# Four of the eight plain weight pieces of an output projection become seven products

## The chip, the cores and the metric

The kernel runs on one core of one Trainium2 chip. The metric is the device time of one execution in microseconds (us). TensorE multiplies, VectorE and ScalarE do the elementwise work, GpSimd's queue (POOL in the profile) issues the adding transfers, and SyncE's queue (SP) issues the plain loads from HBM.

## The reference, cut to what matters

One layer with 256 tokens and a model width of 2048. A first projection feeds two groups of eight heads: `fox` (forgetting attention) and `sb` (stick-breaking attention). Their outputs are normalised group by group and projected, and a gated feed-forward follows:

```
merged = concatenate([rms_norm(out_a, out_norm_fox), rms_norm(out_b, out_norm_sb)])   # 256 x 2048
x = x + merged @ w_out                                                                # w_out 2048 x 2048
x = x + conv_ffn(rms_norm(x, ffn_norm))
```

The change is in `merged @ w_out`, in the part that `out_b` feeds: 256 tokens x 1024 inner x 2048 columns.

## The kernel before

**Three passes for one product.** Every weight piece is 128 partitions x 2048 values. ScalarE writes a rounded copy (`w_hi`, L263) and VectorE the rest (`w_lo = raw - w_hi`, L271). A product is then data high x `w_hi`, data low x `w_hi`, data high x `w_lo`: three matmuls of 512 columns where one would do in full precision. A plain piece of `w_out` covers four heads (4 x 128 inner) and 512 columns, and serves both token tiles: 4 x 3 x 2 = 24 matmuls.

**Seven instead of eight.** For a block of 1024 inner x 1024 columns x 256 tokens the kernel elsewhere uses a scheme of seven products with twelve matmuls each, instead of four plain pieces with twenty-four (84 matmuls for 96). It needs sums of the data blocks, sums of the weight blocks (made by adding transfers on POOL's queue or by VectorE), and one update of `x2` from PSUM for each product. `out_unit` does this for columns 0 to 1023 of the fox heads (group 0).

**The order of work.** The program is a list of steps, one weight piece each. In the iteration of step n the loop at the end of the file emits, in this order: one round of the pending follow-ups (`following`), the split of step n+2's weights, another round of the follow-ups, the load of step n+6, the matmuls of step n, one round of `after` (the transposes), and one tick of the attention heads still running. A follow-up is a generator: each round runs it up to its next `yield`. Each engine works its own instructions strictly in this order. There are five raw weight buffers, three of `w_hi` and three of `w_lo`.

**PSUM.** Eight banks: two double tiles from the pool `psa` (`acc_tile`: plain pieces of the sb heads, later the feed-forward) and a pool `psb` of four single banks with tag `t` (heads, transposes, small sums).

**The stage that is changed.** For the sb heads (group 1) there are eight plain pieces, `out_rows(1, c, kh)`: column block c (512 columns) and head half kh, in the order (0,0) (1,0) (0,1) (1,1) (2,0) (2,1) (3,0) (3,1). Head 7 finishes inside (0,1). After (0,1), `norm_of_heads` turns the sums of squares into the factor `rg1`. Then, once per column block, `follow` adds the two accumulators to `x2` (two VectorE instructions, L989), `next_rows(c)` transposes the finished block on TensorE (eight transposes into two `ps_x` banks, L192), `squares` sums its squares on ScalarE (L210), and `rows_split` evicts the transposes into `hT` as high halves (ScalarE, L200) and low halves (VectorE, L203), one pair of `hT` tiles, a `yield`, then the other pair; after tiles 12 to 15 there is no `yield`. `hT` tiles 4c to 4c+3 are the inner rows of the feed-forward. Its first step uses tiles 0 to 7, its second 8 to 15, in two halves.

Of the kernel before, what the change touches and what calls it, by code (L numbers as in the profile page):

```python
# [45 lines left out]
def hybrid_layer(  # L46
# [731 lines left out]
    def sb_head(h, half):  # L778
# [47 lines left out]
            oSb.append(rows_tile(f"oSb{h}", 0 if h >= 4 else 1, F32R).rearrange("p (a s) -> p a s", a=2))  # L826
        o = oSb[h]
        act.activation(o[:, 0, :], po, AF.Identity, scale=g_sb[:, h : h + 1])
# [36 lines left out]
        ts = slice(t * P, (t + 1) * P)  # L865
        return lambda i, p, _: fox_cells[p][:, 4 * n + i, ts]

    def out_unit(c0):
        w11, w12, w21, w22 = (rows_of(wo, 4 * h, 4, c0 + n * 512, 512) for h in range(2) for n in range(2))
        mem, bank = {}, {}  # L870

        def product(name, new, lhs, weights, to, load_=(), sums=None, plus=None, negative=False, first=False, then=None):
            parts = []
            n, t = to

            def loads():
                for key, src in load_:
                    mem[key] = load(src)
                if plus is not None:
                    nc.gpsimd.dma_start(  # L880
                        mem[weights].rearrange("p (a b) -> p a b", a=4), plus, accum_op=ALU.add
                    )

            def prepare():
                parts.extend(split(mem[weights], 4, 512))

            def matmuls():
                if new:
                    bank[name] = bank_tile(f"bank_{name}", 2 + "ab".index(name[0]))
                in_three([bank[name]], parts, 4, lhs, new, True)  # L890
                if first:
                    following.append(norm_of_heads(0, rgs[0]))
                    next(following[-1])

            def follow():
                while "rg0" not in ready:
                    yield
                xs = x2[:, t, c0 + n * 512 : c0 + (n + 1) * 512]
                r = (nrg0 if negative else rgs[0])[:, t : t + 1]
                dve.scalar_tensor_tensor(xs, bank[name], r, xs, op0=ALU.mult, op1=ALU.add)  # L900
                if then:
                    then()

            new_step(loads, sums, prepare, matmuls, follow)

        def sum_of(other):
            return lambda: dve.tensor_tensor(mem["11"], mem["11"], mem[other], op=ALU.add) and None

        yield product("a", True, of_raw(0, 0), "11", (0, 0), [("11", w11)], first=True)
        yield product("bc", True, of_raw(1, 0), "21", (0, 0), [("21", w21)], then=sum_of("22"))  # L910
        yield product("b", True, fox_sum(T5), "11", (1, 1), [("12", w12)], sum_of("12"))
        yield product("a", False, fox_sum(S2), "11", (1, 0), [("22", w22)], negative=True)
        yield product("b", False, fox_sum(S4), "22", (1, 0))
        yield product("a", False, fox_sum(T7), "12", (1, 1), plus=w22, negative=True)
        yield product("a", False, of_raw(1, 1), "11", (0, 1), plus=w21)

    def split_fox(h):
        act.copy(hT[:, h : h + 4, 0, :], oFox[:, h : h + 4, :])
# [5 lines left out]
    def norm_of_heads(group, rg):  # L924
        pg = psb.tile([P, NT], F32, name="pg", tag="t")
        for t in range(NT):
            nc.tensor.matmul(
                pg[:, t : t + 1], ssq[group][:, t * P : (t + 1) * P], ones[:, 0:1],
                start=t == 0, stop=t == NT - 1,
            )  # L930
        yield
        yield from rsqrt(rg, pg, 1.0 / WF, NT, 2 - group)
        if group == 0:
            dve.tensor_scalar(nrg0, rg, -1.0, None, op0=ALU.mult)
        ready.add(f"rg{group}")

    rgs = [const.tile([P, NT], F32, name=f"rg{i}") for i in range(2)]
    nrg0 = const.tile([P, NT], F32, name="nrg0")
    rstd2 = const.tile([P, NT], F32, name="rstd2")

    def next_rows(c):
# [18 lines left out]
    def out_rows(group, c, kh):  # L960

        def matmuls(parts):
# [14 lines left out]
                middle=finish_heads if flush else middle, apart=1 if flush else 0,  # L977
            )
            if kh == 1 == group and c == 0:
                following.append(norm_of_heads(group, rgs[group]))  # L980
                next(following[-1])

        def follow():
            acc = cells[c]
            while f"rg{group}" not in ready:
                yield
            for t in range(NT):
                xs = x2[:, t, c * 512 : (c + 1) * 512]
                dve.scalar_tensor_tensor(  # L989
                    xs, acc[t], rgs[group][:, t : t + 1], xs, op0=ALU.mult, op1=ALU.add  # L990
                )
            while group == 0 and held:
                held.pop()()
            if group == 1:
                after.append(next_rows(c))
                yield
                if c == 0:
                    spare.append(heads_tile("spare").rearrange("p a b -> p (a b)")[:, :512])
                squares(ss2, c, spare[1])
                if c == 3:  # L1000
                    for _ in token_factors(rstd2, ss2):
                        pass
                    for t in range(NT):
                        dg2.append(R2[:, t * P : (t + 1) * P])
                        dve.tensor_scalar(dg2[t], ident, rstd2[:, t : t + 1], None, op0=ALU.mult)

        pieces(
            wo, group * NH + 4 * kh, 4, 512 * c, 512, matmuls, follow if kh else None,
            held if (group, c, kh) == (0, 3, 0) else None,
        )  # L1010

    dg2 = []
    held = []
    ORDER = [None, (2, 0), None, (2, 1), None, (3, 0), None, None, None, (3, 1), None]
    unit0 = out_unit(0)
# [111 lines left out]
    def up_pieces(part, f0, follows):  # L1127
# [4 lines left out]
        def piece(kh):  # L1132
# [10 lines left out]
            def matmuls():  # L1143
# [1 line left out]
                    cell.append(acc_tile("pu"))  # L1145
                acc, (hi, lo) = cell[0], mem["parts"]
                first = kh and part.f_lo == f0 == 0 and follows is gate_follows
                halves = (range(4), range(4, 8)) if first else (range(8),)
                order = (0, 1) if first else lows
                for ks, low, j in [(ks, low, j) for ks in halves for low in order for j in range(2)]:  # L1150
                        for i in ks:
                            k = 8 * kh + i
                            nc.tensor.matmul(  # L1153
                                acc[:, j, S:] if low else acc[:, j, :],
                                (lo if low else hi)[:, i, j * P : (j + 1) * P],
                                hT[:, k, 0, :] if low else hT[:, k].rearrange("p a b -> p (a b)"),
                                start=k == 0 and not low, stop=k == KT - 1 and low == order[1],
                            )

            new_step(loads, None, prepare, matmuls, (lambda: follows(part, cell[0], f0)) if kh else None)  # L1160
# [174 lines left out]
    def begin(task):  # L1335
        next(task)
        after.append(task)
# [81 lines left out]
```

## Time and profile before

| | |
|---|---|
| three runs, median (lowest to highest) | 1094.4 us (1093.81 to 1095.0) |
| the profiled execution, first to last instruction | 1091.8 us |
| TensorE, VectorE, ScalarE busy | 1087.3, 924.2, 755.1 us |
| granted TensorE clock, mean | 0.999 |
| DMA, mean | 237 GB/s |

The profiled execution has its own time, the span from the first to the last instruction; the runs' time has the launch around it, so the two are compared with their difference in mind. Matmuls overlap, so TensorE's busy share says only that it rarely stands; the chain of waits says when it stands and for whom.

### The profile page before, as it was taken

The page shows a single profiled execution, that of the slowest core. Times are in us where ns is not written, and L with a number is a line of the kernel's source. Part 1 is how long each engine was busy: PE and PEld are TensorE (multiplying, and loading weights), DVE is VectorE, ACT ScalarE, POOL GpSimd, SP SyncE. Part 2 cuts the span into 40 slices and gives each one's busy share as a digit, 9 for nine tenths or more (in the row PEclk, how much of TensorE's full clock was granted, in tenths as well). Part 3 has the DMA queues.
Part 4 walks back from the last instruction along what each step waited for, and adds up shares of the span by engine and source line. Part 5 has one row for each costly group of instructions (what it writes and reads, how often), then busy time and mean ns, then how long its engine had stood idle before and what let it go on. Part 6 is the DMA issues. An engine that isn't in the chain of part 4 may idle for free.

```text
span 1091.8 us, 14685 instructions
## 1 busy us (share of the span) xinstructions
PE 1087.3 (100%) x5701; PEld 939.5 (86%) x5701; DVE 924.2 (85%) x918; ACT 755.1 (69%) x968; POOL 59.0 (5%) x53
## 2 busy tenths in 40 slices
PE   9999999999999999999999999999999999999998
PEld 9988888888888888888888888888888888888887
DVE  5988899888897667779887988889898889879996
ACT  6767697767766657767766776677667767667763
POOL 0000000001000000000000000100000000000000
PEclk9999999999999999999999999999999999999999
DMA  8897886868777465669989597996969799896995
GB/s 310 276 272 239 271 206 196 253 183 271 239 214 251 154 199 161 214 170 249 288 206 316 173 265 254 254 296 170 302 195 271 241 246 279 215 319 161 291 247 155
DMA packets 175215, 258.53 MB, mean 237 GB/s; under 512 B 4632, under 2 KB 98218, under 8 KB 175146
## 3 DMA queue, kind: packets, MB, share of 16 engines
q1 hardware_dynamic: 151690, 210.26, 56.9%
q0 software_dynamic: 23280, 47.19, 24.5%
q8 instruction: 45, 0.74, 0.3%
q14 instruction: 24, 0.20, 0.1%
q10 hardware_dynamic: 176, 0.14, 0.0%
HBM read 255.48 MB, written 2.10 MB: 236 GB/s over the span
## 4 chain that ended last, share of the span: by engine, by line
PE 100%; DVE 0%; issue 0%
PE pu L1153 45%; PE bank_a L291 18%; PE bank_b L291 11%; PE bank_c L291 6%; PE acc_o L291 6%; PE acc_v L411 4%; PE bank_e L291 2%; PE acc L291 2%; PE ps_x L192 1%; PE ps_h L637 1%; PE ps_o L709 1%; PE ps_z L785 0%; PE ps_o L710 0%; PE ps_z L805 0%; PE ps_i L186 0%; PE half L291 0%
## 5 line engine op out<-in xcount | busy, mean ns | idle before, releaser
L271 DVE TENSOR_TENSOR w_lo<-w_raw,w_hi 128x2048 fp32r<-128x2048 f32 (+2 forms) x251 | 555.9, 2219 | 124.1 <-ACT w_hi L263 123.1
L263 ACT CAST w_hi<-w_raw 128x2048 fp32r<-128x2048 f32 (+2 forms) x251 | 464.6, 1854 | 220.7 <-PE pu L1153 90.0
L1153 PE MATMUL pu<-hT,w_hi 128*128 128x512 f32 x1408 | 333.6, 390 | 0.0
L1153 PEld LDWEIGHTS pu<-hT,w_hi 128*128 128x128 f32 x1408 | 263.1, 188 | 53.6
L1153 PEld LDWEIGHTS pu<-hT,w_lo 128*128 128x128 f32 x1408 | 180.0, 191 | 6.5
L1153 PE MATMUL pu<-hT,w_lo 128*128 128x256 f32 x1408 | 182.1, 283 | 0.0
L1206 POOL DMA_DIRECT2D w_raw<-in_w_down_dram x31 | 39.8, 1302 | 715.9 <-DVE w_lo L271 384.7
L1078 ACT ACTIVATE tap<-up,ccol 128x256 f32<-128x256 f32 x176 | 74.6, 495 | 0.0
L291 PE MATMUL bank_a<-w_hi,hT 128*128 128x512 f32 x192 | 48.5, 395 | 0.0
L291 PEld LDWEIGHTS bank_a<-w_hi,hT 128*128 128x128 f32 x192 | 35.2, 188 | 6.7
L291 PE MATMUL bank_b<-w_hi,s 128*128 128x512 f32 x160 | 40.1, 393 | 0.0
L291 PE MATMUL bank_a<-w_hi,s 128*128 128x512 f32 x160 | 40.0, 392 | 0.0
L291 PE MATMUL bank_a<-w_hi,g 128*128 128x512 f32 x152 | 38.0, 392 | 0.0
L411 PE MATMUL acc_v<-w_hi,hT 128*128 128x344 f32 x192 | 35.7, 328 | 0.0
L291 PEld LDWEIGHTS bank_b<-w_hi,s 128*128 128x128 f32 x160 | 28.8, 189 | 5.5 <-issue 0.3
L291 PEld LDWEIGHTS bank_a<-w_hi,s 128*128 128x128 f32 x160 | 28.9, 189 | 5.2
L1083 DVE TENSOR_TENSOR gate<-gate,tap 128x512 f32<-128x512 f32 x44 | 30.3, 689 | 2.7 <-DVE gate L1083 0.5
L1083 DVE TENSOR_TENSOR val<-val,tap 128x512 f32<-128x512 f32 x44 | 30.3, 689 | 2.3
L291 PE MATMUL acc_o<-w_hi,oSb 128*128 128x512 f32 x128 | 31.8, 397 | 0.0
L1064 DVE TENSOR_TENSOR up<-t,R 128x512 f32<-128x512 f32 x44 | 30.5, 692 | 1.5
L291 PEld LDWEIGHTS bank_a<-w_hi,g 128*128 128x128 f32 x152 | 27.4, 189 | 4.9
L411 PEld LDWEIGHTS acc_v<-w_hi,hT 128*128 128x128 f32 x192 | 30.4, 190 | 0.5 <-DVE hT L203 0.2
(293 smaller groups left out, 1411.2 us busy)
## 6 DMA issues: line engine op xcount, KB each, us to landing
w_raw<-in_w_up_dram SPq DMA_DIRECT2D x88, 1024.0 KB, 7.0
w_raw<-in_w_down_dram SPq DMA_DIRECT2D x44, 1024.0 KB, 6.7
w_raw<-in_w_in_dram SPq DMA_DIRECT2D x40, 1024.0 KB, 5.5
w_raw<-in_w_down_dram POOLq DMA_DIRECT2D x31, 1024.0 KB, 9.8
w_raw<-in_w_out_dram SPq DMA_DIRECT2D x16, 1024.0 KB, 7.7
w_raw<-in_w_in_dram POOLq DMA_DIRECT2D x10, 1024.0 KB, 9.4
w_raw<-in_w_in_dram SPq DMA_DIRECT2D x13, 516.0 KB, 5.5
xb<-in_x_dram POOLq DMA_DIRECT2D x4, 512.0 KB, 8.7
```

The source lines that it names most:

```text
L192: nc.tensor.transpose(ps[:, j, t * P : (t + 1) * P], x2[:, t, (k + j) * P : (k + j + 1) * P], ident)
L263: copy(hi[:, :n], raw[:, :n])
L271: dve.tensor_tensor(lo[:, :n], raw[:, :n], f32(hi[:, :n]), op=ALU.subtract)
L291: nc.tensor.matmul(o, lhs(i, l, t), r[:, i, :] if cut is None else r[:, i, cut], start=starts and j == 0, stop=stops and j == 3 * n - 1, s ...
L411: nc.tensor.matmul(banks[j][t][:, :VC], of_half(hT[:, k], l, t), w[:, 0, m * VC : (m + 1) * VC], start=k == l == 0 and w is mem["parts", i ...
L637: nc.tensor.transpose(ps[:, h, :], rows[n, t][:, h * HD : (h + 1) * HD], ident)
L709: mm(po, v, w[:, i, :S], start=m == 0, stop=False)
L1064: dve.tensor_tensor(u[:, :, 2:], t2, R, op=ALU.mult)
L1078: act.activation(taps[w][:, j, :], u[:, j, w : w + S], AF.Copy, scale=ccol[:, w, f : f + 1])
L1083: dve.tensor_tensor(a, a, tap, op=ALU.add)
L1153: nc.tensor.matmul(acc[:, j, S:] if low else acc[:, j, :], (lo if low else hi)[:, i, j * P : (j + 1) * P], hT[:, k, 0, :] if low else hT[: ...
L1206: nc.gpsimd.dma_start(mem[weights].rearrange("p (a b) -> p a b", a=4), plus, accum_op=ALU.add)
```

## The change

It gives columns 1024 to 2047 of the sb heads to `out_unit`, which takes a group, a first column and a function for the raw data tiles now. The eight steps become eleven:

| step | what it multiplies | weights | matmuls |
|---|---|---|---|
| 1 | product a, raw data (heads 0-3, tokens 0-127) | w11 | 12 |
| 2, 3, 4 | plain (0,0), (1,0), (0,1) | own | 24 each |
| 5 | product b, T5 | w11+w12 (adding transfer) | 12 |
| 6 | product bc, raw data (heads 4-7, tokens 0-127) | w21 | 12 |
| 7 | product a, S2 | w11+w12+w22 (VectorE adds w22) | 12 |
| 8 | plain (1,1) | own | 24 |
| 9 | product a, T7 | w12+w22 (adding transfer) | 12 |
| 10 | product b, S4, finishes column block 3 | w22 | 12 |
| 11 | product a, raw data (heads 0-3, tokens 128-255), finishes column block 2 | w11+w12+w22+w21 (adding transfer) | 12 |

The three accumulators a, b and bc come from `psb` (tag `t`). `sb_head` writes heads 4 to 7 once more, whole, into `oFox`; heads 0 to 3 are put together there by VectorE (`sums_of_first_heads`, begun in step 4's iteration). `sums_of_heads` makes the data sums and their high and low halves in five rounds: the first at the end of step 4, with the VectorE sum of w22 into w11 behind it, the others in the rounds of steps 5, 6 and 7. `norm_of_heads` gives `rg1` in one round now. The follow-up of (0,1) has one more `yield` ahead of its two adds and two more behind them. Block 2 is now the last to be finished, so the feed-forward's second step takes tiles 12 to 15 ahead of 8 to 11.

```
+        if h >= 4:
+            act.activation(oFox[:, h, :], po, AF.Identity, scale=g_sb[:, h : h + 1])
...
+        def open_bank(name):
+            if group == 0:
+                return bank_tile(f"bank_{name}", 2 + "ab".index(name[0]))
+            return psb.tile([P, 512], F32, name=f"bank_{name}", tag="t")
...
+        else:
+            yield product("b", True, fox_sum(T5), "11", (1, 1), plus=w12)
+            yield c()
+            weight_sum.append(sum_of("22"))
         yield product("a", False, fox_sum(S2), "11", (1, 0), [("22", w22)], negative=True)
...
+        yield product("a", False, fox_sum(T7), "12", (1, 1), [("12", w12)] if group else (), plus=w22, negative=True)
+        if group:
+            yield s4(3)
+        yield product("a", False, raw_tokens(1, 1), "11", (0, 1), plus=w21, finished=2 if group else None)
...
+        yield from rsqrt(rg, pg, 1.0 / WF, NT, 0 if group else 2)
+        dve.tensor_scalar(nrgs[group], rg, -1.0, None, op0=ALU.mult)
...
             if kh == 1 == group and c == 0:
-                following.append(norm_of_heads(group, rgs[group]))
+                following.extend((norm_of_heads(group, rgs[group]), sums_of_heads()))
+                next(following[-2])
                 next(following[-1])
...
+            if group > c:
                 yield
             for t in range(NT):
                 xs = x2[:, t, c * 512 : (c + 1) * 512]
...
+            if group > c:
+                yield
+                yield
             if group == 1:
-                after.append(next_rows(c))
...
+                yield from columns_done(c)
...
+    def sums_of_heads():
+        a11, a21 = oFox[:, first_heads, first_tokens], oFox[:, first_heads, last_tokens]
+        a12, a22 = oFox[:, last_heads, first_tokens], oFox[:, last_heads, last_tokens]
+        dve.tensor_tensor(a21, a21, a22, op=ALU.subtract)
+        high_sum(first_heads, last_tokens)
+        dve.scalar_tensor_tensor(a22, a11, -1.0, a22, op0=ALU.mult, op1=ALU.subtract)
+        low_sum(first_heads, last_tokens)
+        weight_sum.pop()()
+        yield
+        high_sum(last_heads, last_tokens)
+        low_sum(last_heads, last_tokens)
+        dve.tensor_tensor(a12, a12, a22, op=ALU.add)
+        yield
+        high_sum(last_heads, first_tokens)
+        high_sum(first_heads, first_tokens)
+        yield
+        low_sum(first_heads, first_tokens)
+        yield
+        yield
+        low_sum(last_heads, first_tokens)
...
-    for c, kh in ((0, 0), (1, 0), (0, 1), (1, 1), (2, 0), (2, 1), (3, 0), (3, 1)):
-        out_rows(1, c, kh)
+    SB_OUT = len(steps)
+    unit1 = out_unit(1, 1024, of_heads)
+    for what in (None, (0, 0), (1, 0), (0, 1), None, None, None, (1, 1), None, None, None):
+        if what is None:
+            next(unit1)
+        else:
+            out_rows(1, *what)
...
-                halves = (range(4), range(4, 8)) if first else (range(8),)
+                halves = (range(4, 8), range(4)) if first else (range(8),)
...
+    hooks[SB_OUT + 2] = lambda: following.append(sums_of_first_heads())
```

`high_sum` is a ScalarE copy and `low_sum` a VectorE subtraction of 128 x 512 values; `columns_done` holds what stood at the end of `follow` (transposes, squares, and after the last block the token factors).

More of the change, by code (lines that the diff above doesn't have):

```diff
@@ L888, in matmuls @@
                 if new:
-                    bank[name] = bank_tile(f"bank_{name}", 2 + "ab".index(name[0]))
+                    bank[name] = open_bank(name)
                 in_three([bank[name]], parts, 4, lhs, new, True)
@@ L902, in follow @@
                     then()
+                if finished is not None:
+                    yield from columns_done(finished)
             new_step(loads, sums, prepare, matmuls, follow)
@@ L1156, in matmuls @@
                                 hT[:, k, 0, :] if low else hT[:, k].rearrange("p a b -> p (a b)"),
-                                start=k == 0 and not low, stop=k == KT - 1 and low == order[1],
+                                start=k == 0 and not low, stop=bool(kh) and k == last_k and low == order[1],
                             )
```

77 lines of the change are left out of this document (50 added, 27 removed).

## The prediction

> **What bounds the kernel now.** I read the page's busy shares and its chain first, then the chain in order of time through the stage, then the busy time by stretch, then VectorE's timeline. TensorE is the whole chain:
>
> ```profile
> span 1091.8 us, 14685 instructions
> PE 100%; DVE 0%; issue 0%
> ...
> 314.73 2.75 PE bank_a L291 x12
> ...
> 340.98 5.52 PE acc_o L291 x24
> ...
> 347.60 0.98 PE acc_o L291 x4
> 348.58 0.43 PE ps_o L821 x2
> 349.01 0.22 PE ps_o L822 x2
> 349.23 4.58 PE acc_o L291 x20
> 353.81 0.34 PE pg L927 x4
> ...
> 366.25 0.87 PE ps_x L192 x8
> ...
> 384.38 5.54 PE pu L1153 x32
> 389.92 0.87 PE ps_x L192 x8
> 390.79 5.59 PE pu L1153 x32
> ```
>
> A product of 12 matmuls takes 2.75 us, a plain piece of 24 takes 5.5, with nothing between them. So a matmul left out is worth its 0.229 us, and any time for which TensorE stands is lost whole. The question is whether VectorE can still feed it:
>
> ```profile
> 284.70:334.40 49.70, 49.70 (x244) 41.78 (x244) 48.29 (x55) 35.21 (x43) 2.60 (x2) 1.00 0.77 228
> 334.40:384.40 50.00, 50.00 (x244) 41.80 (x243) 34.12 (x47) 29.75 (x48) 0.00 (x0) 1.00 0.53 173
> ...
> PEld ps_x L192 <- DVE xb L989: 0.3, 1, 0.3
> ```
>
> The columns are stretch, length, busy us of TensorE, weight loads, VectorE, ScalarE, POOL, then clock and DMA. The first row holds the seven products of the fox heads: VectorE is busy for 48.29 of 49.70 us there, and TensorE doesn't stand. The second row is the stage that changes: 34.12 of 50.00. The last row matters most: TensorE already waits 0.3 us for the adds of column block 0 ahead of their transposes. There is no slack at that place.
>
> **What is saved.** Four plain pieces (96 matmuls) become seven products (84): 12 x 0.229 = 2.7 us less on TensorE. Transposes and feed-forward matmuls keep their number.
>
> **What VectorE gets, and its prices.**
>
> ```profile
> 308.24 4.49 DVE L271 TENSOR_TENSOR w_lo<-w_raw,w_hi 128x2048 fp32r<-128x2048 f32 x2
> ...
> 350.45 0.41 DVE L834 TENSOR_TENSOR ssq<-ssq,osq 128x256 f32<-128x256 f32 x1
> 354.19 0.16 DVE L168 TENSOR_SCALAR rs_a<-pg 128x2 f32<-128x2 f32 x1 [3.32 <-PE pg L927]
> ...
> 357.55 0.15 DVE L173 TENSOR_TENSOR rs_u<-rs_a,rs_y 128x2 f32<-128x2 f32 x1
> 357.73 0.16 DVE L174 TENSOR_TENSOR rs_u<-rs_u,rs_y 128x2 f32<-128x2 f32 x1
> ...
> 358.33 1.41 DVE L989 SCALAR_TENSOR_TENSOR xb<-acc_o,rg,xb 128x512 f32<-128x512 f32 x2
> 361.35 0.88 DVE L203 SCALAR_TENSOR_TENSOR hT<-ps_x,pcol,hT 128x256 fp32r<-128x256 f32 x2 [1.61 <-ACT hT L200]
> ...
> L907 DVE TENSOR_TENSOR w_raw<-w_raw 128x2048 f32<-128x2048 f32 x2 | 4.6, 2282 | 0.0
> L853 DVE TENSOR_TENSOR oFox<-oFox 128x512 f32<-128x512 f32 x1 | 0.7, 694 | 0.0
> ```
>
> Two splits last 4.49 us while one row is 2.29: behind one another, an instruction starts 0.09 us before the row ahead of it ends. Queue prices are then: split or weight sum 2.20, update of `x2` 0.66 (from the pair of 1.41), `hT` low half 0.40, a sum of 128 x 512 0.60, the 128x2 steps of the norm 0.20. Added: three splits 6.6, one weight sum 2.2, three updates 2.0, seven sums in `sums_of_heads` 4.2, the sums of the first heads 1.9 (four of half width, one of 0.60). That is 16.9 us on 34.1, in a stage of 47.3: over 100% before any wait. So what counts is where the overflow lies in the strict order.
>
> **The place: transposes of block 0.** I walk the queues from head 7. Up to (0,1) the new stage has 12 matmuls more (12+24+24 for 24+24), so (0,1) starts at 347.60 + 2.75 = 350.35. TensorE then has 24 matmuls with head 7's 0.65 between them, the 0.34 of `pg`, and steps 5 and 6: 350.35 + 0.98 + 0.65 + 4.58 + 0.34 + 5.5 = 362.4. There the transposes of block 0 are due. VectorE's last work on head 7 began 2.85 us after (0,1)'s start (350.45 - 347.60); with the extra `oFox` copy ahead of it on ScalarE (0.36, estimated from the row of 0.47 below) it is free for the sums at 353.9. In emission order follow: three sums with a wait for ScalarE's copy (2.0), the weight sum (2.2), the norm (six small steps and ScalarE's two, 1.7), two sums (1.2), the split for step 7 with its wait for the cast (2.4), the update of step 1 and the two adds of (0,1) (2.0). That is 11.5 us: 365.5. The adds stand behind all of it since the added `yield` lets the split go first. **TensorE waits 3.1 us** where it waited 0.3 (ends 2.1 and 3.6: the queue without its small waits, and with as much again on ScalarE's side); nothing hides it, since step 7 is queued behind these transposes. The first sums do not hurt: step 5 needs them at 356.9 and has them at 355.9.
>
> **The second place: the banks.** `psb` has four banks. When `next_rows(0)` is emitted, behind step 6, a, b and bc hold three: bc's update comes only in step 7's iteration. The eight transposes need two. The second four must wait until the first bank is given back, which is behind the low halves of the first pair. VectorE's queue up to there: a sum 0.60, the update of step 5 0.66, the split for step 8 2.20, a sum 0.60, two low halves 0.88: 4.9 us, 370.4, against 366.0 when the first four transposes are through: **4.4 us**. The trace has only short waits of this kind:
>
> ```profile
> PEld ps_h L637 <- ACT kB L641: 0.2, 1, 0.2
> ```
>
> Zero is the lower end (if the allocation finds a bank), 5.1 the upper (if it is bc's bank that comes free, one update later); I take 4.4, since the pair's bank is given back first.
>
> **Then it catches up.** Step 8 is long, and VectorE is through its splits before (1,1) ends. From there VectorE has, up to the add that finishes block 3: two adds 1.3, two splits 4.4, four low halves 1.6, two updates 1.3 and about 1.0 of waits for ScalarE: 9.6 us, beside 9.1 of TensorE (three products and eight transposes 0.87). It waits **0.9 us** ahead of block 3's transposes (0.5 by the plain difference; the rest is the lag of matmul ends).
>
> **The last place: block 2 in the feed-forward's second step.** These rows are of block 1 and of the last block in before:
>
> ```profile
> 366.72 0.84 ACT L200 ACTIVATE hT<-ps_x,pcol 128x256 fp32r<-128x256 f32 x2 [1.51 <-PE ps_x L192]
> 367.45 1.91 ACT L263 CAST w_hi<-w_raw 128x2048 fp32r<-128x2048 f32 x1
> ...
> 369.39 2.29 DVE L271 TENSOR_TENSOR w_lo<-w_raw,w_hi 128x2048 fp32r<-128x2048 f32 x1 [0.92 <-ACT w_hi L263]
> 371.60 0.87 DVE L203 SCALAR_TENSOR_TENSOR hT<-ps_x,pcol,hT 128x256 fp32r<-128x256 f32 x2
> ...
> 390.39 1.57 ACT L200 ACTIVATE hT<-ps_x,pcol 128x256 fp32r<-128x256 f32 x4 [1.62 <-PE ps_x L192]
> 391.27 1.66 DVE L203 SCALAR_TENSOR_TENSOR hT<-ps_x,pcol,hT 128x256 fp32r<-128x256 f32 x4 [1.11 <-ACT hT L200]
> ```
>
> The last block was evicted in one go (x4: tiles 12 to 15 have no `yield`), done 3.0 us after its transposes began (392.93 - 389.92). Block 2 is last now, and its tiles 8 to 11 do have the `yield`: a cast and a split stand between the pairs, as in block 1, where the second pair's first low half is done at 371.60 + 0.48, 5.8 us after 366.25. The second step needs tile 10 after 0.87 + 2.8 (half the step) + 0.46 (two matmuls) = 4.1 us. At least 1.7 us are missing. And block 3's four pairs, now at the head of the first step, push the cast and split behind them, the token factors after these, and ScalarE's two small instructions for the factors stand ahead of block 2's first pair: some 1.1 us more, by the same queue count. I take **3.1 us** with 0.2 for the first pair; ends 1.7 and 3.3.
>
> **What costs nothing.**
>
> ```profile
> L263 ACT CAST w_hi<-w_raw 128x2048 fp32r<-128x2048 f32 x24 | 45.8, 1906 | 14.8 <-PE acc_o L291 7.2 <-DVE w_raw L907 3.1 <-DMA w_raw<-in_w_out_dram 2.0
> L918 ACT CAST hT<-oFox 128x1024 fp32r<-128x1024 f32 x2 | 2.1, 1052 | 0.6 <-PE bank_a L291 0.6
> L828 ACT ACTIVATE oSb<-ps_o,pcol 128x256 fp32r<-128x256 f32 x8 | 3.7, 468 | 1.5 <-PE ps_o L822 1.0 <-PE ps_o L710 0.5
> ...
> w_raw<-in_w_out_dram POOLq DMA_DIRECT2D x2, 1024.0 KB, 9.2
> ```
>
> ScalarE gets three casts, four copies of half of L918's width and four of L828's kind: about 9.5 us on 29.75, not full; where it delays VectorE, that is counted above. Three adding transfers come on POOL's queue, 9.2 us each to landing. The last (w21 into w11) can start when the split for step 7 is done, 363.6, lands at 373, and is wanted by the cast of step 11 after 376: 3 us of cover; without it step 11 would come that much later. SP's queue has eight loads as before, now for eleven steps; w11, w12 and w22 keep their buffers longer, but by the emission order no more than five are held at once, so the feed-forward's loads behind them find theirs in time. The first sums (1.9 us) lie in idle time of VectorE ahead of head 7. If that cover failed they would add 1.9 to the first wait.
>
> **The sum.** Waits 3.1 + 4.4 + 0.9 + 3.1 = 11.5; less 2.7 saved, less the old wait of 0.3: +8.5 us. On the profiled span 1091.8 that gives 1100.3. The runs' median is 2.6 above that span, so 1094.4 becomes 1102.9; I say 1103.0. Less than 0.2% (2.2 us) is about what a measurement of this kernel can't tell from no change.
>
> A rule that speaks against the change: the Trainium skill, "TensorE: Matmul & The Clock Gate", Part 1, says that TensorE's clock falls to half after an idle window of about 3.4 us and takes about as long to return. By it the sum would be about 1.7 us more, an estimate from that figure (half of 3.4). Neither stretch above shows it, as both have clock 1.00 and no such gap.
>
> **Rivals.**
> - *The banks don't collide.* A bank is found for the second four transposes. The 4.4 go, but VectorE's backlog then shows later: from 353.9 to the add that finishes block 3 it has 30.6 us of queue by the prices above (seven of 2.20, seven sums, ten updates, eight low halves, the norm) and 1 of waits, so that add ends at 385.5. TensorE's own work from 362.4 to there is steps 7 to 11 (four products 11.0, one plain piece 5.5) and the transposes of blocks 0 and 1 (1.7): 380.6, so it stands 4.9 us in all. With 3.1 in the feed-forward and 2.7 + 0.3 off: +5.0, 1099.4.
> - *VectorE keeps up: faster.* The fox stage ran at 97% without a stand, since low halves are wanted 1.8 us later than high ones (behind 8 matmuls of a product). If the adds of block 0 were done by 362.4, at 8.5 us of queue instead of 11.5, and tile 10 in time, the whole 2.7 is gained: 1091.7. It decides at the first transposes. Against it stands the 0.3 us row.
> - *Even.* The first wait of 3.1 is all that comes and eats the saving: 1094.5.
> - *The clock falls.* Two waits with only 0.4 us of transposes between them make 7.5 us. If the granted clock halves for one product behind it, 2.75 us more: 1105.7. The page named above gives this mechanism; no row here has it.
>
> **How the numbers follow.** Forecast 0.50; no collision 0.22; clock 0.10; faster 0.10; even 0.08. The first three are slower: 0.82. Same 0.08, faster 0.10. The range leaves out the last two: from the no-collision case with the lower end of the feed-forward wait (1099.4 - 1.4 = 1098.0) to the clock case (1105.7) with a little for the lag of ends: 1098.0 to 1106.0.
>
> **What would show it.** TensorE's instructions fall by 12. Its waits list `ps_x` behind `xb` with about 3, `ps_x` behind `hT` with over 4, and `pu` behind `hT` with about 3 near 400; VectorE is busy for over 95% of the time from head 7 to step 8. I am wrong if block 0's transposes follow step 6 within half a us, or all eight run in one go, or the second feed-forward step takes 5.6 us.

## The result and the profile after

The changed kernel took 1106.84 us (median of four runs, 1105.94 to 1107.3), beside 1094.11 for the kernel before on the same chip (1093.56 to 1095.0). The ratio is 1.0114, with a 95% interval of 1.0099 to 1.0128. So it is slower, as forecast, by 12.7 us instead of 8.5, and outside the range.

The page of the changed kernel: its span and busy times, and the chain's shares by engine.

```profile
span 1105.4 us, 14705 instructions
...
PE 1091.1 (99%) x5689; PEld 940.0 (85%) x5689; DVE 942.0 (85%) x938; ACT 763.8 (69%) x979; POOL 62.8 (6%) x56
...
PE 94%; DVE 2%; ACT 1%; issue 1%; DMA 1%; SPq 1%; ACTq 0%; DVEq 0%
```

The chain was TensorE alone before. Now VectorE, ScalarE and the queues hold some per cent of it. Most of the rest of the story is in one stretch, from 362 to 411 us. TensorE's timeline of the changed kernel there; the columns are start, length, the instructions, and in brackets the idle time ahead of them with what ended it:

```profile
362.92 1.07 PE L291 MATMUL bank_bc<-w_lo,oSb 128*128 128x512 f32 x4
366.40 0.40 PE L192 MATMUL ps_x<-cs,xb 128*128 128x128 f32 x1 [2.40 <-issue]
367.01 0.90 PE L192 MATMUL ps_x<-cs,xb 128*128 128x128 f32 x3 [0.21 <-DVE xb L1015]
371.94 1.09 PE L192 MATMUL ps_x<-cs,xb 128*128 128x128 f32 x4 [4.03 <-DVE hT L203]
372.68 3.76 PE L291 MATMUL bank_a<-w_hi,hT 128*128 128x512 f32 x8
...
377.39 3.79 PE L291 MATMUL acc_o<-w_hi,oSb 128*128 128x512 f32 x16
...
392.66 1.09 PE L192 MATMUL ps_x<-cs,xb 128*128 128x128 f32 x8 [0.60 <-DVE xb L909]
393.51 3.92 PE L1233 MATMUL pu<-hT,w_hi 128*128 128x512 f32 x16
...
402.85 0.63 PE L1233 MATMUL pu<-hT,w_hi 128*128 128x512 f32 x2
405.80 1.99 PE L1233 MATMUL pu<-hT,w_hi 128*128 128x512 f32 x6 [2.32 <-DVE hT L203]
407.58 1.91 PE L1233 MATMUL pu<-hT,w_lo 128*128 128x256 f32 x8
...
410.66 3.98 PE L1233 MATMUL pu<-hT,w_hi 128*128 128x512 f32 x16
```

Four stands are to be seen, and all four end on VectorE: block 0's adds, the bank for its second four transposes, block 3's add, and tile 10 in the feed-forward's second step. For the first of them the profile names no releaser (`issue`); the transpose starts at 366.40, just behind the first of the two adds below (365.55 and 0.75, as an update takes alone, is 366.30). The bank wait has no name of its own; it shows as TensorE waiting for the eviction (`hT`) of the pair whose bank it takes. VectorE's timeline of the changed kernel says why:

```profile
357.49 2.29 DVE L918 TENSOR_TENSOR w_raw<-w_raw 128x2048 f32<-128x2048 f32 x1
...
362.68 2.29 DVE L271 TENSOR_TENSOR w_lo<-w_raw,w_hi 128x2048 fp32r<-128x2048 f32 x1 [0.17 <-ACT w_hi L263]
364.89 0.75 DVE L909 SCALAR_TENSOR_TENSOR xb<-bank_a,rg,xb 128x512 f32<-128x512 f32 x1
365.55 1.40 DVE L1015 SCALAR_TENSOR_TENSOR xb<-acc_o,rg,xb 128x512 f32<-128x512 f32 x2
...
368.13 2.28 DVE L271 TENSOR_TENSOR w_lo<-w_raw,w_hi 128x2048 fp32r<-128x2048 f32 x1
...
370.93 0.87 DVE L203 SCALAR_TENSOR_TENSOR hT<-ps_x,pcol,hT 128x256 fp32r<-128x256 f32 x2
...
403.06 2.29 DVE L271 TENSOR_TENSOR w_lo<-w_raw,w_hi 128x2048 fp32r<-128x2048 f32 x1 [0.40 <-ACT w_hi L263]
405.27 0.87 DVE L203 SCALAR_TENSOR_TENSOR hT<-ps_x,pcol,hT 128x256 fp32r<-128x256 f32 x2
```

The weight sum, the split and the update stand ahead of the adds, which end at 366.95 (365.55 + 1.40); another split stands ahead of the low halves that free the bank, and a third ahead of tile 10's.

What the forecast did not have in its sum is the clock. Busy time by stretch of the changed kernel (stretch, length, TensorE, weight loads, VectorE, ScalarE, POOL, clock, DMA share, GB/s):

```profile
366.46:369.88 3.42, 1.24 (x4) 0.55 (x4) 3.42 (x4) 3.25 (x7) 0.28 (x1) 0.50 0.73 105
...
373.29:376.70 3.41, 3.41 (x10) 2.64 (x9) 2.15 (x3) 0.84 (x3) 0.00 (x0) 0.50 1.05 339
404.01:407.42 3.41, 1.62 (x6) 1.18 (x7) 2.13 (x3) 0.00 (x0) 0.00 (x0) 1.00 1.09 354
407.42:410.84 3.42, 3.42 (x19) 3.31 (x18) 0.42 (x1) 2.38 (x2) 0.00 (x0) 0.50 0.97 308
```

The clock is at half from 366.46 for three stretches of 3.41 us, and again from 407.42 for one. In the kernel before the clock was 1.00 here. The second and the fourth row show what it costs: TensorE is busy throughout, and a matmul of 512 columns takes 0.445 us from start to start (3.56 for eight, from 372.68 to 376.24 in the full timeline) where it took 0.229. The third row is the stretch ahead of the second fall; TensorE was busy for 1.62 us of it and stood for the rest.

For the account, some rows of TensorE's timeline of the kernel before:

```profile
334.15 2.99 PE L291 MATMUL acc_o<-w_hi,oSb 128*128 128x512 f32 x12
...
384.22 3.79 PE L1153 MATMUL pu<-hT,w_hi 128*128 128x512 f32 x16
...
396.92 0.48 PE L1153 MATMUL pu<-hT,w_hi 128*128 128x512 f32 x1
```

Worked out from starts, which the modelled ends don't blur:

| term | us | from |
|---|---|---|
| ahead of the stage | +1.5 | first product of the sb heads at 335.67 for 334.15; 0.2 of it is there at 54 us already |
| 12 matmuls fewer, old wait gone | -3.0 | 12 x 0.229, and the 0.3 |
| block 0's adds | +3.1 | 362.92 + 0.92 to 366.40, and 0.5 behind the first transpose |
| the bank | +4.4 | 367.01 + 0.55 (three transposes at 0.185) to 371.94 |
| block 3 | +0.8 | against the end of the product ahead of it, 391.9 |
| tile 10 | +2.5 | 402.85 + 0.46 to 405.80 |
| clock at half, first | +2.5 | product a 4.71 (372.68 to 377.39) for 2.75; seven transposes at 0.185 for 0.11 |
| clock at half, second | +1.9 | 393.51 to 410.66 is 17.15 for 12.70 in before, less the 2.5 of tile 10 |
| together | +13.7 | up to 410.66, where before had 396.92; the whole span grew by 13.6, the runs by 12.7 |

### The profile page after: what moved, and what is told of

Its sections match the earlier page's. It is cut to its first block, busy times and chain, and to the rows that moved or that the text cites. A ratio compares the mean times of both kernels' runs of the same rounds, so it can differ in the third digit from the quotient of the medians.

```text
span 1105.4 us, 14705 instructions
## 1 busy us (share of the span) xinstructions
PE 1091.1 (99%) x5689; PEld 940.0 (85%) x5689; DVE 942.0 (85%) x938; ACT 763.8 (69%) x979; POOL 62.8 (6%) x56
## 4 chain that ended last, share of the span: by engine, by line
PE 94%; DVE 2%; ACT 1%; issue 1%; DMA 1%; SPq 1%; ACTq 0%; DVEq 0%
PE pu L1233 43%; PE bank_a L291 19%; PE bank_b L291 10%; PE bank_c L291 6%; PE acc_v L411 3%; PE acc_o L291 3%; PE bank_e L291 2%; PE acc L291 2%; ACT w_hi L263 1%; PE ps_h L637 1%; DMA w_raw<-in_w_in_dram 1%; PE ps_o L709 1%; DVE w_lo L271 0%; SPq L257 0%; PE ps_x L192 0%
## 5 line engine op out<-in xcount | busy, mean ns | idle before, releaser
L271 DVE TENSOR_TENSOR w_lo<-w_raw,w_hi 128x2048 fp32r<-128x2048 f32 (+2 forms) x254 | 562.9, 2220 | 117.5 <-ACT w_hi L263 116.8
L263 ACT CAST w_hi<-w_raw 128x2048 fp32r<-128x2048 f32 (+2 forms) x254 | 470.3, 1854 | 223.3 <-PE pu L1233 94.2
L291 PE MATMUL bank_a<-w_hi,hT 128*128 128x512 f32 x208 | 54.3, 404 | 0.0
L291 PEld LDWEIGHTS bank_a<-w_hi,hT 128*128 128x128 f32 x208 | 39.2, 194 | 7.7
L1150 ACT ACTIVATE gate<-up,ccol 128x256 f32<-128x256 f32 x44 | 24.1, 594 | 11.0 <-DVE s L1204 5.5
```

Source lines behind the costliest of these rows:

```text
L263: copy(hi[:, :n], raw[:, :n])
L271: dve.tensor_tensor(lo[:, :n], raw[:, :n], f32(hi[:, :n]), op=ALU.subtract)
L291: nc.tensor.matmul(o, lhs(i, l, t), r[:, i, :] if cut is None else r[:, i, cut], start=starts and j == 0, stop=stops and j == 3 * n - 1, s ...
L1150: act.activation(a[:, j, :], u[:, j, 2:], AF.Identity, scale=ccol[:, 2, f : f + 1], bias=ccol[:, 3, f : f + 1],)
```

## The experiments

The theories that the expectations name: **A**, the prediction's places (VectorE's strict queue, the banks, block 2's `yield`), each with the clock fall behind its stand. **B**, the clock falls for a reason of its own. **C**, the waits are for weights and transfers. **D**, VectorE's added work is the bound wherever it lies. **L**, the added constant tile `nrg1` (128 x 2) shifts what lies behind it in on-chip memory and slows the part ahead of the stage. **R**, that part varies from run to run. All times are medians in us; before is the kernel before in the same job. It moves by 0.4 us from job to job, so a difference between two jobs is good to about that much.

| run | time | before | ratio, 95% |
|---|---|---|---|
| the change | 1106.84 | 1094.11 | 1.0114 [1.0099, 1.0128] |
| e1_evict_at_once | 1102.78 | 1093.72 | 1.0083 [1.0068, 1.0098] |
| e2_fill_second_step | 1105.80 | 1093.72 | 1.0108 [1.0093, 1.0123] |
| e3_two_rounds_of_transposes | 1102.64 | 1093.72 | 1.0082 [1.0067, 1.0097] |
| e4_weight_sum_by_transfer | 1105.72 | 1093.72 | 1.0109 [1.0092, 1.0125] |
| e5_const_only | 1095.06 | 1093.80 | 1.0011 [1.0002, 1.0020] |
| e6_all_three | 1098.00 | 1093.80 | 1.0042 [1.0028, 1.0055] |
| e7_no_new_constant | 1097.69 | 1093.80 | 1.0037 [1.0024, 1.0051] |
| e8_sums_on_gpsimd | 1097.65 | 1093.80 | 1.0038 [1.0024, 1.0051] |
| e9_shared_only | 1105.49 | 1094.09 | 1.0107 [1.0091, 1.0122] |
| e10_behind_step_7 | 1096.77 | 1094.09 | 1.0023 [1.0013, 1.0033] |
| e11_and_gpsimd | 1094.60 | 1094.09 | 1.0008 [1.0000, 1.0017] |
| e12_two_rounds_too | 1094.31 | 1093.90 | 1.0003 [0.9994, 1.0012] |

### Block 2 evicted in one go (e1)

```
-            if k < KT - 4:
+            if k < KT - 8:
                 yield
```

> The changed kernel, with block 2's four tiles evicted in one go (no yield behind tiles 8 to 11). Theory A (order of the queues, banks, and a clock that halves behind a long wait): the wait of 2.5 us in the feed-forward's second step goes down to some 0.3, and the half clock from 407.4 to 410.8 us, which costs 1.8, does not come: 4.0 us less, 1102.8. Theory B (the clock falls for a reason of its own): 2.2 us less, 1104.6, half clock still there. Theory C (the step waits for its weights): no change, 1106.8.

Measured 1102.78, 4.1 less than the change (3.7 against the kernel before of each job). TensorE's timeline of this run, and its busy time by stretch:

```profile
402.68 2.15 PE L1233 MATMUL pu<-hT,w_hi 128*128 128x512 f32 x8
```

```profile
400.00:410.00 10.00, 10.00 (x57) 8.49 (x56) 8.70 (x16) 5.96 (x9) 0.00 (x0) 1.00 0.98 315
```

The eight matmuls of the second step's high half run in one go, where the change ran two and stood. The stand and the clock fall behind it both go, at the place that A named, for an edit that leaves weights and transfers as they were: A's 1102.8 came, and not the 1104.6 of B or the 1106.8 of C.

### The wait kept, TensorE kept busy (e2)

Eleven matmuls into a bank that nothing reads are put in where the second step waits for tile 10. The wait stays, but TensorE doesn't stand.

```
+                            if first and k == 10 and not low and not j:
+                                spare_bank = psb.tile([P, 512], F32, name="spare_bank", tag="t")
+                                for m in range(11):
+                                    nc.tensor.matmul(spare_bank, ...)
```

> The changed kernel, with eleven idle matmuls of 512 columns (2.5 us, into a bank that nobody reads) at the place where the feed-forward's second step waits 2.5 us for tile 10. Theory A: TensorE is busy through the wait, so the granted clock stays at 1.00 there; the wait itself is only filled: 1.8 us less, 1105.0. Theory B: half clock from 407 to 411 us all the same, no change, 1106.8 (or later by what the fill overshoots).

Measured 1105.80. TensorE's timeline of this run, and its busy time by stretch:

```profile
405.81 1.86 PE L1240 MATMUL pu<-hT,w_hi 128*128 128x512 f32 x6
407.51 1.12 PE L1240 MATMUL pu<-hT,w_lo 128*128 128x256 f32 x8
```

```profile
401.00:415.00 14.00, 14.00 (x82) 12.01 (x81) 8.96 (x14) 7.05 (x8) 0.00 (x0) 1.00 0.82 260
```

Tile 10's matmuls start at 405.81, where the change had 405.80, and the clock stays at 1.00; the eight matmuls of the low half take 1.12 instead of 1.91. So the fall belongs to the stand, and B falls for this place. By the median the gain is 1.0, less than A's 1.8, and 0.65 against the kernel before of each job; by the spans of the two profiled executions it is 1.6 (1103.8 for 1105.4). So the effect on the clock is shown, its size in the runs only roughly.

### Block 0's transposes in two rounds (e3)

```
+        if c == 0:
+            for k in (0, 2):
+                following.append(rows_split([(k, transposed(k))]))
+                yield
+            return
```

> The changed kernel, with block 0's transposes in two rounds of four, the second four behind step 7 instead of ahead of it, so that bc's bank is back when they need it. Theory A: the wait of 4.0 us on the banks goes, VectorE's backlog shows later instead (some 1.0 us more at the transposes of blocks 1 and 3), and with one wait of 2.5 to 3 us left the clock falls for one window of 3.4 us at most, not for three: 3.4 + 1 to 2 us less, 1101.9 (1101 to 1103.5). Theory C (step 7 waits for its weights or for adding transfers, not for a bank): no change, the same 4 us ahead of step 7's matmuls.

Measured 1102.64. TensorE's timeline of this run, and its busy time by stretch:

```profile
367.47 2.10 PE L291 MATMUL bank_a<-w_hi,hT 128*128 128x512 f32 x8
...
372.10 0.63 PE L192 MATMUL ps_x<-cs,xb 128*128 128x128 f32 x4 [1.63 <-DVE hT L203]
```

```profile
365.16:368.57 3.41, 1.71 (x9) 1.37 (x10) 3.41 (x6) 2.54 (x7) 1.29 (x1) 1.00 0.30 24
...
399.29:402.70 3.41, 1.71 (x6) 1.24 (x7) 2.04 (x3) 0.00 (x0) 0.00 (x0) 1.00 1.09 352
402.70:406.11 3.41, 3.41 (x18) 3.40 (x17) 0.44 (x2) 2.38 (x2) 0.00 (x0) 0.50 0.96 305
```

Step 7 now runs between the two fours of transposes; the bank wait shrinks from 4.03 to 1.63 (A had expected it gone) and the first clock fall is gone. So the place was the bank, as A had it, and not weights or transfers (C). The gain of 4.2 us (3.8 against the kernel before of each job) is the bank wait and the fall behind it taken together; this run doesn't part them. The rows also show a limit of what can be said: the first and the second stretch shown have the same busy time, 1.71; behind the second the clock fell (the row below it), behind the first it stayed at 1.00. And of the four runs of this kernel, one (1101.65) had a mean clock of 1.000, so not even the second fall came there.

### The weight sum as an adding transfer (e4)

```
-            weight_sum.append(sum_of("22"))
+                    nc.gpsimd.dma_start(mem[weights]..., behind, accum_op=ALU.add)
```

VectorE's addition of w22 is left to POOL's queue, behind the split of step 5.

> The changed kernel, with w22 added into w11 by a fourth adding transfer on POOL's queue, behind the split for step 5, instead of by VectorE (2.2 us in its queue ahead of block 0's adds). Theory A: the adds of block 0 come only 1.0 us sooner, since the norm then waits for TensorE's sums and the split for its cast; the bank wait stays: 1.0 us less, 1105.8, with the same two falls of the clock. Theory D (VectorE's work is all that counts, wherever it lies): 2.2 us less, 1104.6. If transfers are the bound, later.

Measured 1105.72. TensorE's timeline of this run:

```profile
365.18 0.30 PE L192 MATMUL ps_x<-cs,xb 128*128 128x128 f32 x1 [1.14 <-issue]
...
370.73 1.09 PE L192 MATMUL ps_x<-cs,xb 128*128 128x128 f32 x4 [4.39 <-DVE hT L203]
```

Block 0's transposes come 1.2 earlier (366.40 in the change), and so does the bank, with a wait of 4.39 for 4.03. The 2.2 us instruction was worth 1.1: on VectorE the norm, which had stood behind it, now waits 0.87 us for TensorE's sums (`pg`). A's 1105.8 came, and not D's 1104.6.

### The constant tile alone (e5, e9)

e5 is the kernel before with the tile added and never read; e9 is the change with one tile shared by both groups, so that none is added.

```
+    nrg1 = const.tile([P, NT], F32, name="nrg1")
+    dve.memset(nrg1, 0.0)
```

```
-    rgs, nrgs = ([const.tile([P, NT], F32, name=f"{n}{i}") for i in range(2)] for n in ("rg", "nrg"))
+    rgs = [const.tile([P, NT], F32, name=f"rg{i}") for i in range(2)]
+    nrgs = [const.tile([P, NT], F32, name="nrg0")] * 2
```

> The kernel before with one more constant tile of 128 x 2 values (set to zero, read by nobody), as the changed kernel has it, and nothing else of the change. In the changed kernel's trace TensorE is 1.5 us late when the first product of the sb heads begins, though the instructions up to there are the same; the delay grows evenly from 54 to 290 us. Theory L (the tile shifts all later tiles' places, and that slows the first half): 1.5 us more, 1095.2, with the same even growth. Theory R (one execution differs from another by so much): no change, 1093.7.

> The changed kernel with the negative factors of both groups in one tile, so that the constants keep the size they have in the kernel before; nothing else. Theory A with L (the shifted places cost 1.2 us ahead of the stage): 1.2 us less, 1105.6, no growing delay between 54 and 290 us, the waits and half clocks of the stage as they are. Theory R: no change, 1106.8.

Measured 1095.06 in e5, 1.26 more than before, and 1105.49 in e9, 1.35 less than the change. The same 230 us of busy time by stretch, far ahead of the stage, in the kernel before, e5 and e9 in this order:

```profile
60.00:290.00 230.00, 230.00 (x1108) 193.21 (x1107) 200.20 (x215) 170.25 (x272) 14.42 (x13) 1.00 0.82 241
```

```profile
60.00:290.00 230.00, 230.00 (x1103) 192.06 (x1102) 199.03 (x214) 170.02 (x272) 14.42 (x13) 1.00 0.82 241
```

```profile
60.00:290.00 230.00, 229.98 (x1108) 193.14 (x1107) 200.20 (x215) 170.45 (x272) 14.43 (x13) 1.00 0.82 241
```

With the tile TensorE gets through 1103 matmuls, without it through 1108, at clock 1.00 and without a stand. All fourteen traces here fall into the same two groups: 1103 or 1104 in the seven kernels with the tile (the change, e1 to e6), 1108 in the seven without it (before, e7 to e12). Five matmuls are 1.0 us at the mean of this stretch (230 / 1108 = 0.208). The offset against before grows along the way: in e5, counted from 57 us on, it is 0.6 at 174 us and 1.2 at 288. R falls, and L holds as far as the tile goes; that it works by shifting what lies behind it is not shown.

### All cures together (e6, e7)

e6 has e1 and e4, and block 0's transposes behind step 8; e7 also shares the constant tile and puts the norm ahead of the other follow-ups.

```
-                yield
-                yield
+                for _ in range(6):
+                    yield
```

```
-                following.extend((norm_of_heads(group, rgs[group]), sums_of_heads()))
-                next(following[-2])
+                following.insert(0, norm_of_heads(group, rgs[group]))
+                following.append(sums_of_heads())
+                next(following[0])
```

> The changed kernel with the three cures together: block 2 evicted in one go, w22 added into w11 by an adding transfer, and block 0's transposes behind step 8 instead of step 6. Theory A: no wait on banks, none of 2.5 us in the feed-forward, no half clock; left are waits of about 1 us each ahead of step 7, of block 1's and of block 3's transposes, since VectorE has more queue than TensorE has matmuls: 1.3 us over the kernel before, and the 1.4 that come ahead of the stage: 1096.5 (1095.5 to 1098). Theory D (VectorE's work is the bound wherever it lies): not under 1099. If the cures only swap waits: 1102.

> The kernel with the three cures, with the negative factors of both groups in one tile (so that no tile is added to the constants), and the norm ahead of step 1's update in the round, so that this update no longer stands behind the split for step 7. Theory A with L: the 1.4 us ahead of the stage go, and 0.7 of the wait ahead of step 7: 1094.4. Theory A with R: 0.7 less than with the three cures.

Measured 1098.00, at the upper end of A's range around 1096.5 and under D's 1099, and 1097.69 where 1094.4 was expected. From e6 to e7 the median gains 0.3 of the 2.1 that A with L had; by the spans of the two profiled executions it is 1.1 (1095.0 for 1096.1), and the gap between the two readings stays open. The waits of e7 (engine, what, releaser: us in total, times, longest):

```profile
PE ps_x L192 <- DVE hT L203: 2.5, 1, 2.5
```

The bank wait has moved, not gone: in e6 and e7 it stands ahead of block 1's second four transposes, with the clock at half for 3.41 us behind it. Blocks 0 and 1 come close together there, and each wants two banks.

### VectorE's sums on GpSimd (e8)

```
+        low_sum(last_heads, last_tokens, nc.gpsimd)
+        nc.gpsimd.tensor_tensor(a12, a12, a22, op=ALU.add)
...
+        low_sum(first_heads, first_tokens, nc.gpsimd)
...
+        low_sum(last_heads, first_tokens, nc.gpsimd)
```

> The kernel of the run before in this list (three cures, no new constant), with four of the seven data sums and low halves on GpSimd, which takes 2.4 us out of VectorE's queue. Theory A: 1.0 us less, 1093.4, so that the seven products come out at about the time of the kernel before or 0.1% under it, if a sum of 128 x 512 takes GpSimd up to 2 us. If GpSimd takes more than 3 us for one, step 7 waits for its data: later.

Measured 1097.65, no gain on e7: the bank wait at block 1 is 3.57 now. GpSimd's timeline of this run, and one row of VectorE's:

```profile
355.84 1.64 POOL L1078 TENSOR_TENSOR oFox<-oFox 128x512 f32<-128x512 f32 x1 [4.78 <-DVE oFox L1073]
358.42 1.30 POOL L1057 TENSOR_TENSOR hT<-oFox,hT 128x512 fp32r<-128x512 f32 x1 [0.95 <-ACT hT L1054]
360.75 4.47 POOL L1057 TENSOR_TENSOR hT<-oFox,hT 128x512 fp32r<-128x512 f32 x2 [1.03 <-ACT hT L1054]
```

```profile
358.46 1.28 DVE L176 TENSOR_TENSOR rg<-rs_y,rs_u 128x2 f32<-128x2 f32 x1
```

A sum takes 1.30 to 2.24 us there (4.47 / 2) where VectorE took 0.69. Much of the relief is lost on the way: a step of VectorE's norm takes 1.28 us (the row) where e7 has 0.16, and ends with GpSimd's sum of 358.42; a split beside the later sums takes 2.67 where e7 has 2.28. Together that is 1.5 of the 2.4 us, the same in e11 and e12, and in none of the runs without GpSimd's sums; that the sums cause it is not shown. At block 1 what is left of the relief doesn't arrive: the split ahead of the low halves waits 0.95 us for ScalarE's cast and starts at 376.13, in e7 at 376.22.

### Block 0's transposes behind step 7, then GpSimd, then two rounds (e10, e11, e12)

e10 is e7 with four rounds in the place of six; e11 adds e8's edit, e12 adds e3's to that.

```
-                for _ in range(6):
+                for _ in range(4):
                     yield
```

> Four cures (block 2 evicted in one go, weight sum by transfer, norm ahead of step 1's update, no new constant) with block 0's transposes behind step 7 instead of step 8. Behind step 8, their two banks were not back when block 1's transposes came behind step 9 (2.6 us in the three runs with the cures, which I had not counted). Theory A: with one plain step between them no bank is waited for; waits of 0.6 to 1.6 us at steps 8 and 9 are left from VectorE's queue, no half clock: 0.5 us over the kernel before, 1094.3 (1093.8 to 1095.5). If the backlog only moves: 1097 again.

> The same with four of the seven data sums and low halves on GpSimd, 2.4 us out of VectorE's queue; a sum takes GpSimd 1.3 to 2.2 us in the run that had this. Theory A: 0.7 us less than without it, 1093.6, even with the kernel before or just under it. Theory D' (VectorE isn't the bound any more): no difference between the two.

> The kernel with the four cures and GpSimd sums, in which TensorE still waits 2.2 us for the bank that bc gives back (block 0's second four transposes behind step 7), and the clock still halves for one window behind it. Here the second four come behind step 8, when that bank is long free. Theory A: the 2.2 go and the half window with its 1.7 us: 3.9 less than 1094.6, 1090.7, if VectorE's queue doesn't show that time again ahead of block 1's and block 3's transposes; with as much as 1 us there, 1091.7. That would be 0.2 to 0.3% under the kernel before: the gain of the twelve matmuls, for the first time. Theory D (VectorE's backlog only moves): 1094.5 again.

Measured 1096.77, 1094.60 and 1094.31; A had expected 1094.3, 1093.6 and about 1091. In the traces of e10 and e11 the second four transposes wait for the bank of product bc, 3.05 us and 2.16, with the clock at half for 3.41 us behind it. Not every run of these two kernels has that fall, which shows in the mean clock as 0.998 (3.41 us at half in 1095). In e10, five of eight runs have 0.997 or 0.998 and take 1096.61 to 1097.82, and three have 1.000 and take 1095.11 to 1095.74; in e11, four of eleven have 0.998, at 1095.58 and above, while the others, at 0.999 or 1.000, take 1094.66 or less. So the same kernel differs by 1.4 to 1.8 us with and without one fall, and each median mixes the two. Among runs without it, GpSimd's sums gain 0.8 (1095.35 for e10, 1094.53 for e11), about A's 0.7. Against the 1094.53, e12 gains only 0.2, though e11's trace has a bank wait of 2.16 that e12 is rid of: the time shows again elsewhere, as D had it. TensorE's timeline of e10:

```profile
369.49 1.11 PE L192 MATMUL ps_x<-cs,xb 128*128 128x128 f32 x4 [3.05 <-DVE xb L913]
```

In e12 no bank is waited for, and the clock is 1.00 throughout. TensorE's timeline of e12, and one row of VectorE's:

```profile
373.28 1.07 PE L291 MATMUL bank_a<-w_lo,hT 128*128 128x512 f32 x4
374.99 0.30 PE L192 MATMUL ps_x<-cs,xb 128*128 128x128 f32 x1 [0.63 <-issue]
375.60 0.99 PE L192 MATMUL ps_x<-cs,xb 128*128 128x128 f32 x7 [0.31 <-DVE xb L1023]
...
381.41 1.08 PE L291 MATMUL bank_a<-w_lo,oSb 128*128 128x512 f32 x4
383.30 1.09 PE L192 MATMUL ps_x<-cs,xb 128*128 128x128 f32 x8 [0.81 <-DVE xb L913]
384.14 3.90 PE L1240 MATMUL pu<-hT,w_hi 128*128 128x512 f32 x16
```

```profile
374.15 1.39 DVE L1023 SCALAR_TENSOR_TENSOR xb<-acc_o,rg,xb 128x512 f32<-128x512 f32 x2
```

```profile
353.85:376.70 22.85, 21.90 (x106) 17.73 (x105) 21.26 (x27) 15.72 (x22) 8.63 (x5) 1.00 0.89 208
```

Four matmuls take 0.92 from start to start, so TensorE stands 0.8 ahead of block 1's transposes, 0.5 behind the first of them, 0.3 ahead of step 11 and 1.0 ahead of block 3's transposes: 2.6 us, all but the 0.3 released by VectorE's adds. That is what the seven products saved (2.7). The feed-forward starts at 384.14 where before had 384.22. The last fence, busy time by stretch, has the reason: VectorE is busy for 21.26 of 22.85 us, though GpSimd does four of its sums (7.4 of GpSimd's 8.63 us). In its timeline VectorE never stands for more than 0.2 us at a time from 359.42 to 385.4, and the adds at 374.15, for which block 1's transposes wait, come in the middle of that. A missed here and D's 1094.5 was right: with every misplaced wait cured, VectorE's queue eats the saving, what GpSimd's sums seem to add to it included. Twelve and a half us were taken out of the change, and what is left is even with before, not faster. That the work is too much in every order is not shown; only these orders were run.

## Why the prediction missed its range

**What held.** The bound, the direction and all four places. VectorE's queue from head 7 was walked to 365.5 and ended at 366.95, 1.5 late because it began 1.6 late (355.51 for 353.9); its length was forecast at 11.5 and came at 11.4. The waits, forecast against measured: block 0's adds 3.1 and 3.1, the bank 4.4 and 4.4, block 3 0.9 and 0.8, tile 10 3.1 and 2.5. Together 11.5 and 10.8. Net of the saving and the old wait, 8.5 was forecast and 7.8 came. e1, e3 and e4 confirm three of the places, each with an edit at the place; block 3's 0.8 us had no run of its own.

**What failed: the clock, which the sum takes at nothing.** The prediction saw it, priced it as a rival at one fall of 2.75, gave it 0.10, and left it out of the sum because no row of before has a stand that long. But its own forecast contained two long stands: 7.5 us with 0.4 us of transposes in them, and 3.1 us at tile 10, for which it considered no fall at all. The clock fell behind both, for 2.5 and 1.9, 4.4 us in all; the rival's 2.75 was about the price of the first. With a forecast of such stands, the falls should have been in the sum. The Trainium skill, "TensorE: Matmul & The Clock Gate", Part 1, gives the rule for it: half clock after one idle window of about 3.4 us. Here the rows of 3.41 us agree with the window's length. They do not bear out a window that is idle throughout: the second fall came behind a stand of 2.5 us, in a stretch with TensorE busy for 1.62.

**What was not seen: 1.5 us ahead of the stage.** The prediction has the stage begin when it began in before; it did not look at the added tile, a 128 x 2 constant. e5 and e9 price it at 1.3 us on its own; the other 0.2 stood at 54 us already. The tile's being there is shown to be the cause; what it does to the matmuls, which take half a per cent longer, is open.

**The rivals.** That the banks don't collide is refuted by the change itself and e3. Even and faster were not what the change as it stood gave; e12 comes out even, but only with seven edits and by another way than the rival, which had one wait of 3.1 us. In e12 it is VectorE's full queue, which the prediction had put first as its 16.9 us more.

Adding up, 7.8 + 4.4 + 1.5 = 13.7, against 13.6 of the span. The forecast of 8.5 had the first term alone. The upper end of the range, 1106.0, had room for one fall and no more; without the tile the change takes 1105.49 (e9), so it took the falls and the tile together to leave it.

## What to carry to other kernels

A saving of matmuls can be worth nothing, as in e12, where the engine that pays for it is nearly full: add the added work up per stage on the engine's strict queue, then walk the queue to each place where TensorE is due. When that walk forecasts a stand of some 2.5 us or more, put the fall of the clock into the sum as well, for each stand (here 1.9 and 2.5 us, though not in every run), and look first at what can be moved so that a long product runs between two waits (e3) or an eviction isn't cut in two by a split (e1). A wait for a bank shows as a wait for the eviction of some other tile, and curing it in one place can move it to the next user of the pool (e7, e10).

## What the runs showed of the hardware that was not expected

- The granted clock halves for whole stretches of 3.41 us, and one stretch partly idle is enough: 1.62 busy of 3.41 ahead of 407.42 in the change, 1.71 of 3.41 ahead of 402.70 in e3. With the grid of 3.41 us on which the falls lie laid over all fourteen traces from 345 to 420 us, 14 of the 15 stretches at full clock in which TensorE was busy for 1.75 us or less were followed by half clock, and none of those with 1.91 or more (none lies between). The one exception is e3's stretch from 365.16, with 1.71. So half of a stretch is about the line, by busy time as the profile models it, and the same wait can meet the grid in another way in another run: e3, e6, e10 and e11 have runs with and without a fall. That the place on the grid decides there is likely, not shown, since the traces here are of one run of each.
- Idle matmuls in the gap keep the clock at 1.00 (e2).
- One constant tile of 128 x 2 values that nothing reads makes the kernel 1.3 us slower (e5), spread over the first 290 us.
- GpSimd's sums of 128 x 512 values took 1.30 to 2.24 us, VectorE's 0.69. Beside them a VectorE step on 128 x 2 values took 1.28 us for 0.16 (e8, e11, e12).
